# Pairing the sliding-window heads of an even block on both row halves of TensorE

## The chip, the core and the metric

The kernel runs on one core of a Trainium2 chip. A core has TensorE (PE, with its weight loads shown apart as PEld), VectorE (DVE), ScalarE (ACT), GpSimd (POOL) and a queue engine (SP) that only issues DMAs here. The metric is the device time of one execution in microseconds; the numbers given are medians over runs.

## The reference

Four layers run one after another on x of 512 tokens by 1024 channels, in float32: an even attention block, an odd attention block, a convolution block and a gated recurrent block, the last two each followed by an MLP. The change is in the even block alone:

```python
z = h @ w_in          # splits: cq 384, ckv 256, kr 32, sq 512, sk 128, sv 128, gate 1024
o_mla = mla_attention(q_nope, q_rope, k_nope, k_rope, v_mla)      # 8 heads, causal, 512 channels
q_s = apply_rope(z_sq.reshape(b, s, 8, 64)); k_s = apply_rope(z_sk.reshape(b, s, 2, 64))
o_swa = swa_sink_attention(q_s, k_s, v_s, sinks)                  # 8 heads of 64, window 128
o = jnp.concatenate([o_mla, o_swa], axis=-1) * jax.nn.silu(z_gate)
y = o @ w_out
```

In the sliding-window attention (SWA) heads 0 to 3 share the first key and value head and heads 4 to 7 the second. A query block of 128 tokens sees its own and the previous block, and a sink joins the softmax's sum.

## The kernel before

Matrices are multiplied as three products each: both operands are split into a high and a low part, and high*high, high*low and low*high are added up in PSUM (`mm3`, L206). `wgran` (L210) loads a piece of a weight by a DMA on SP's queue into `raw` (4 buffers), ACT copies the high part and DVE or POOL subtracts to get the low part into `hl` (5 buffers).

o lies transposed, eight chunks of 128 channels by 512 tokens: chunks 0 to 3 hold the MLA heads in pairs, 4 to 7 the SWA heads in pairs. `gates` (L703) computes one chunk of silu(z_gate) into o: eight steps of three products of 512 columns, then Tanh on ACT and one DVE operation. When a chunk's attention is done, `pv_out` (L690) multiplies it in.

Attention is a generator that yields after each step: one pair of heads and one query block. A step computes the scores of either head (`scores`, L694, three products into one of two PSUM tiles "sc"), the softmax (`softmax`, L629: a DVE pass with mask and minimum, Exp on ACT, a reciprocal on DVE, the scaling on POOL), the transposes of the probabilities on PE (`p_T`, L662, copied out by ACT), and the products with V (`pv_pair`, L680, two heads side by side on column halves).

`mla()` has 16 steps, with 128 to 512 keys; `swa()` has 16 steps, with 128 or 256 keys. In SWA before the change the pairs are heads (0,1), (4,5), (2,3), (6,7). Queries are stored as tiles that hold head i on partitions 0 to 63 and head i+4 on partitions 64 to 127, keys likewise; a step of before uses two such tiles and one row half of each, and V of one key head for both.

`weave` (L260) mixes a main generator with fill, which is here the gates of chunks 1 to 3, the key and value product (`ev_sk`), and the gates of chunks 4, 6, 5, 7. After step i it lets the fill go on until a cost of `cost*(i+1)/n` units is issued; a gate's step of three products counts 1, a step of the key product 0.5. What it issues for step i may not run before the last PE instruction of step i-FD (`behind`, with `FD = 6`); for i < FD there is no such hold:

```python
marks.append(self.last(self.pe))
with self.behind(marks[-1 - FD] if i >= FD and FD >= 0 else None):
    have = self.advance(fill, have, want(i + 1) - 1e-6)
```

The first weave spends `W_MLA` = 52 units on MLA, the second the rest of 76 on SWA. The order of the instructions on each engine is fixed when the program is built, by a planner that simulates the time line and takes what is ready by priority; on the chip each engine runs its list in that order. Modulation sums for later layers (`ada`, DVE lines L544 and L546, 512 KB loads on SP's queue) are released by `tick` at the ends of gates and heads. After SWA, `out_first` (L734) splits o and multiplies it with w_out (`gemm_tb`, L318), whose rows are in the order of o's channels.

Of the kernel before, what the change touches and what calls it, by code (L numbers as in the profile page):

```python
# [16 lines left out]
P = 128  # L17
# [3 lines left out]
KC = D // P  # L21
EPS = 1e-6
BIG = 1e30
TERMS = ((0, 0), (0, 1), (1, 0))
# [5 lines left out]
C_SM = C_CM + 512  # L30
# [9 lines left out]
STRICT = 0  # L40
FD = 6
ADA_OFF = 0
W_MLA = 52
ONDVE = (0, 1, 2)
W_FOX = 3
MAIN_OFF = 0
# [18 lines left out]
SQF = 0  # L65
G0 = 2
# [41 lines left out]
def cap4(v, o):  # L108

    return bass.AP(tensor=v.tensor, offset=v.offset + o, ap=[[P, 4], [0, 32], [1, P]])  # L110


class K:
# [96 lines left out]
    def wgran(self, w, k0, nk, c0, cw, own=False):  # L210

        n = nk * cw
        raw = self.wp.tile([P, 1024], F32, tag="raw", name=self.nm("raw"), bufs=4)
        self.nc.sync.dma_start(
            out=raw[:, :n].rearrange("p (k c) -> p k c", c=cw),
            in_=w[k0 * P:(k0 + nk) * P, c0:c0 + cw].rearrange("(k p) c -> p k c", p=P))
        if own:
            hl = self.work("hl2", [P, 2, 1024], F32R)
        else:
            hl = self.wp.tile([P, 2, 1024], F32R, tag="hl", name=self.nm("hl"), bufs=5)  # L220
        hi, lo = hl[:, 0, :n], hl[:, 1, :n]
        self.nc.scalar.copy(out=hi, in_=raw[:, :n])  # L222
        self.wn += 1
        eng = self.nc.gpsimd if self.lo_pool and self.wn % self.lo_pool == 0 else self.nc.vector
        eng.tensor_tensor(out=lo, in0=raw[:, :n], in1=hi.bitcast(F32), op=ALU.subtract)  # L225
        return hl[:, :, :n].rearrange("p a (k c) -> p a k c", c=cw)
# [33 lines left out]
            have += c  # L260
        return have

    def weave(self, main, n, fill, cost):


        have, marks = 0, []
        want = cost if callable(cost) else lambda i: cost * i / n
        for i in range(n):
            with self.rank(-MAIN_OFF):
                next(main)  # L270
            marks.append(self.last(self.pe))
            with self.behind(marks[-1 - FD] if i >= FD and FD >= 0 else None):
                have = self.advance(fill, have, want(i + 1) - 1e-6)
        self.run(main)

# [418 lines left out]
    def scores(self, rows, q, k, qb, k0, n, extra=None):  # L694
# [5 lines left out]
            self.nc.tensor.matmul(ps[:, :n], lhsT=A[:, qb * P:(qb + 1) * P], rhs=Bh[:, k0:k0 + n], start=False, stop=True)  # L700
        return ps

    def gates(self, act, w, c0, o, cs):  # L703

        nc = self.nc
        for c in cs:
            def e(m, ps, oc=o[:, c, :]):
                nc.scalar.activation(out=oc, in_=ps, func=AF.Tanh, scale=0.5)
                nc.vector.scalar_tensor_tensor(out=oc, in0=oc, scalar=1.0, in1=ps, op0=ALU.add, op1=ALU.mult)
            yield from self.gemm_ws(act, w, c0 + c * P, P, KC, e)  # L710
# [54 lines left out]
    def even(self, act, gs):  # L765
        nc, h = self.nc, self.h
        w = h["ev_w_in"][0]
# [36 lines left out]
        SV = self.work("SV", [P, NTB, P])  # L804
# [9 lines left out]
        o = self.otile()  # L814
# [7 lines left out]
        for c in range(5):  # L822
            ps = self.psum("tp")
            for tb in range(NTB):
                nc.tensor.transpose(ps[:, tb * P:(tb + 1) * P], lat[tb][:, c * P:(c + 1) * P], self.ident)
            s = self.vcol("ev_q_norm", c) if c < 3 else self.vcol("ev_kv_norm", c - 3)
# [10 lines left out]
        V = [self.work("V", [P, 512]) for _ in range(NTB)]  # L837
# [49 lines left out]
        def swa():  # L887
            self.npool = NPL[1]
            t = self.tmp()[:, :512].rearrange("p (tb d) -> p tb d", d=P)
            nc.scalar.dma_start(out=t, in_=sqd[:, 8:10, :].rearrange("(tb p) n d -> p tb (n d)", p=P))  # L890
            kT = self.heads_T(t, 128, lambda s, tb: s[:, tb])

            def load(i):
                t = self.tmp()[:, :512].rearrange("p (tb r d) -> p tb r d", r=2, d=64)
                for r in range(2):
                    nc.scalar.dma_start(out=t[:, :, r, :], in_=sqd[:, i + 4 * r, :].rearrange("(tb p) d -> p tb d", p=P))
                return self.heads_T(t, 128, lambda s, tb: s[:, tb].rearrange("p r d -> p (r d)"), -0.125)

            qTs = {0: load(0), 1: load(1)}
            for hd in (0, 4, 2, 6):  # L900
                r = hd // 4
                pv = self.psum("pv")
                for qb in range(NTB):
                    k0 = max(0, qb - 1)
                    nb = qb - k0 + 1
                    n = nb * P
                    ps = []
                    for h_ in (hd, hd + 1):
                        sc = self.scores(slice(64 * r, 64 * r + 64), qTs[h_ % 4], kT, qb, k0 * P, n)
                        ps.append(self.softmax(sc, n, self.cst[:, C_SM + 256 - n:C_SM + 256], sink=self.nsink[:, h_:h_ + 1]))  # L910
                    self.pv_pair(pv, [[SV[:, b, r * 64:r * 64 + 64] for b in range(k0, qb + 1)]] * 2, ps, qb)
                    if hd == 4 and qb < 2:
                        qTs[qb + 2] = load(qb + 2)
                    yield
                self.tick(TSW)
                self.pv_out(o[:, 4 + hd // 2, :], pv)

        def fill():
            if SQF:
                yield from self.gates(act, w, 1440, o, (0, 1)[G0:])  # L920
                yield from self.gemm_xs(act, w, 1184, 256, KC, ev_sk)
                yield from self.gates(act, w, 1440, o, (2,))
                yield from self.gemm_xs(act, w, 672, 512, KC, ev_sq)
                yield from self.gates(act, w, 1440, o, (3, 4, 6, 5, 7))
                return
            yield from self.gates(act, w, 1440, o, (1, 2, 3))
            yield from self.gemm_xs(act, w, 1184, 256, KC, ev_sk)
            yield from self.gates(act, w, 1440, o, (4, 6, 5, 7))

        self.lo_pool = LOP[0]  # L930
        if not SQF:
            self.run(self.gates(act, w, 1440, o, (0,)))
        g = fill()
        self.weave(mla(), 16, g, W_MLA + 16 * SQF)
        self.weave(swa(), 16, g, (96 - 8 * G0 if SQF else 76) - W_MLA)
        return o


# [710 lines left out]
def build(tc, h, upto=99):  # L1649
    nc = tc.nc  # L1650
    with ExitStack() as es:
        k = K(tc, h, es)
        k.epsc = k.cp.tile([P, 1], F32, name="epsc")
        nc.vector.memset(k.epsc, EPS)
        x_in = h["x"][0]
        out = h["out"][0]
        x1 = k.dp.tile([T, D], F32, name="x1")
# [4 lines left out]
        with k.scope(t4=5, xn=1, SB=2, wide=8, wsb=2, rep=1, prow=1, col=1):  # L1662
            cc, cc2, act, gs = k.start(x_in, h["c"], h["c_2"], wa[0], ba[0], h["g_pre"][0], h["ev_w_in"][0], 384)
# [30 lines left out]
                        k.mark()  # L1694
                    return o

        act = first(0, lambda a: k.even(a, gs), act, x_in, out if upto == 1 else x1, h["ev_w_out"][0], t4=4, ru=1, s=6, pt=6, b4=6, V=4, SV=1)
        if upto == 1:
            return
        act = first(1, k.odd, act, x1, out if upto == 2 else x2, h["od_w_out"][0], t4=2, ru=1, hn=1, s=6, pt=6, b4=4, Vd=4, V=4, foxA=1, foxB=1, foxBh=2, lp=1)  # L1700
# [63 lines left out]
        with tc.tile_pool(name="xp", bufs=1, reuse_waits="tile") as k.xp:  # L1764
            act, xr = second(0, act, k.conv, x2, t4=4, u=3, dw=1, dwr=1, w4=1, u4=4, dg=3)
# [27 lines left out]
        with tc.tile_pool(name="xp", bufs=1, reuse_waits="tile") as k.xp:  # L1793
            act, xr = second(1, act, k.hgrn, x4, V=8, X=3, F=1, op=2, hn=1, gt=1, AT=1, Ad=2, T0=1, T1=1, T2=1, T3=1, T4=1, T5=1, T6=1)
# [41 lines left out]
```

## Time and profile before

| | |
|---|---|
| median of 3 runs | 2090.42 us (2090.31 to 2091.31) |
| profiled execution | 2096.67 us, of which its span, first to last instruction, is 2094.5 us |
| mean granted TensorE clock | 0.964 of full speed |
| busy: PE, DVE, ACT, POOL | 94%, 65%, 41%, 36% of the span |

The rows of the next section are from that profiled execution. Times there are microseconds from the start of the span. An engine is busy while it executes; matmuls are pipelined, and the ends shown overlap the next one, so that the time of a run of products is best read from its start to the start of what follows.

### The profile page before, as it was taken

What the parts mean: (1) busy time and instruction counts of PE and PEld (TensorE: products, weight loads), DVE (VectorE), ACT (ScalarE), POOL (GpSimd) and SP (SyncE); (2) the same over time, 40 slices, a digit from 0 to 9 for tenths busy, and PEclk for the clock granted to TensorE, in tenths of its full rate; (3) what the DMA queues carried; (4) which work ended last, traced back from release to release, by engine and by line L of the source; (5) the groups of instructions that cost most, each with busy time, mean ns of one, the idle gap of its engine ahead of it and who ended that gap; (6) DMA issues with size and microseconds to landing.
All of it is one profiled execution on the core that took longest, in us unless ns stands there. A gap on an engine that the chain in (4) does not pass through costs nothing. (4 is left out here: it accounts for less than half of the span.)

```text
span 2094.5 us, 33197 instructions
## 1 busy us (share of the span) xinstructions
PE 1958.5 (94%) x13047; PEld 1598.5 (76%) x13047; DVE 1356.8 (65%) x1992; ACT 862.1 (41%) x1465; POOL 745.2 (36%) x671
## 2 busy tenths in 40 slices
PE   7799999689999999889899999999989998999998
PEld 5687767677766787458787989877777678898896
DVE  4356774467553379546987648668777958475673
ACT  4245542235543342143525436244445534353452
POOL 1233334233233333006242322456666443323232
PEclk9899979899999999989999999999999999999999
DMA  8475456377761335832555225353313422242331
GB/s 306 134 211 154 131 175 150 80 173 166 116 149 50 129 123 187 226 82 80 174 166 165 80 91 181 127 150 109 100 58 113 132 81 72 90 131 71 121 100 62
DMA packets 229971, 272.12 MB, mean 130 GB/s; under 512 B 26810, under 2 KB 154009, under 8 KB 229816
## 3 DMA queue, kind: packets, MB, share of 16 engines
q1 hardware_dynamic: 192054, 232.83, 38.5%
q10 hardware_dynamic: 37762, 37.18, 6.0%
q8 instruction: 103, 1.69, 0.3%
q14 instruction: 52, 0.43, 0.1%
HBM read 253.57 MB, written 16.40 MB: 129 GB/s over the span
## 5 line engine op out<-in xcount | busy, mean ns | idle before, releaser
L208 PE MATMUL mm<-hTh,hl 128*128 128x512 f32 (+2 forms) x1200 | 371.8, 384 | 0.1
L222 ACT CAST hl<-raw 128x1024 fp32r<-128x1024 f32 (+3 forms) x219 | 224.2, 1033 | 242.3 <-PE mm L208 121.4
L208 PE MATMUL mm<-hl,hid 128*128 128x512 f32 x1344 | 317.4, 395 | 3.6 <-DVE hid L201 2.0
L208 PEld LDWEIGHTS mm<-hl,hid 128*128 128x128 f32 x1344 | 251.7, 188 | 64.0 <-DVE hid L201 2.8
L225 DVE TENSOR_TENSOR hl<-raw,hl 128x1024 fp32r<-128x1024 f32 (+2 forms) x187 | 246.6, 1328 | 56.2 <-ACT hl L222 55.5
L208 PEld LDWEIGHTS mm<-hTh,hl 128*128 128x128 f32 (+1 forms) x1200 | 217.4, 188 | 49.0 <-issue 6.5
L208 PE MATMUL mm<-hl,hTh 128*128 128x256 f32 (+3 forms) x848 | 220.9, 342 | 31.5 <-DVE t L625 20.6
L208 PE MATMUL mm<-hTl,hl 128*128 128x512 f32 (+2 forms) x600 | 229.3, 382 | 0.1
L208 PEld LDWEIGHTS mm<-hl,hTh 128*128 128x128 f32 x848 | 153.6, 202 | 49.0 <-issue 15.0
L1148 POOL TENSOR_TENSOR xr<-xr,t 128x512 f32<-128x512 f32 x56 | 80.9, 1445 | 307.8 <-DVE t L1145 307.8
L644 POOL TENSOR_TENSOR s<-s,sm 128x256 f32<-128x256 f32 (+3 forms) x112 | 80.6, 720 | 201.0 <-DVE sm L640 192.7
L546 DVE SCALAR_TENSOR_TENSOR acc<-araw,ccol,acc 128x512 f32<-128x512 f32 x154 | 134.8, 875 | 26.6 <-DMA araw<-in_ada_w_dram 20.6
L208 PE MATMUL mm<-hl,hTl 128*128 128x256 f32 (+3 forms) x424 | 143.3, 338 | 0.7 <-DVE hTl L458 0.7
L200 ACT CAST hl<-raw 128x1024 fp32r<-128x1024 f32 x84 | 86.8, 1048 | 138.5 <-PE mm L208 111.9
L201 DVE TENSOR_TENSOR hl<-raw,hl 128x1024 fp32r<-128x1024 f32 x84 | 131.4, 1579 | 13.8 <-ACT hl L200 13.2
L208 PEld LDWEIGHTS mm<-hTl,hl 128*128 128x128 f32 (+1 forms) x600 | 112.9, 188 | 22.0 <-issue 1.7
L1211 POOL TENSOR_TENSOR raw<-raw,raw 128x1024 f32<-128x1024 f32 x28 | 77.1, 2752 | 143.1 <-DVE rows L1211 89.2
L225 POOL TENSOR_TENSOR hl<-raw,hl 128x1024 fp32r<-128x1024 f32 x32 | 80.9, 2529 | 88.6 <-ACT hl L222 88.5
L1145 DVE TENSOR_TENSOR t<-mm,rows 128x512 f32<-128x512 f32 x56 | 38.5, 688 | 108.7 <-PE mm L208 108.3
L639 ACT ACTIVATE s<-s,sm 128x256 f32<-128x256 f32 (+5 forms) x128 | 69.6, 544 | 90.1 <-DVE sm L637 83.5
L1596 POOL TENSOR_TENSOR X<-X,T 128x512 f32<-128x512 f32 x56 | 76.3, 1368 | 58.0 <-ACT op L1556 45.1
L208 PE MATMUL sc<-b,b 64*128 64x256 f32 (+7 forms) x384 | 92.0, 356 | 1.7 <-DVE sm L637 1.3
(366 smaller groups left out, 4060.0 us busy)
## 6 DMA issues: line engine op xcount, KB each, us to landing
raw<-in_mlp_w_dram SPq DMA_DIRECT2D x128, 512.0 KB
araw<-in_ada_w_dram SPq DMA_DIRECT2D x72, 512.0 KB
raw<-in_hgrn_w_in_dram SPq DMA_DIRECT2D x40, 512.0 KB
araw<-in_w_ada_dram SPq DMA_DIRECT2D x32, 512.0 KB
raw<-in_od_w_in_dram SPq DMA_DIRECT2D x32, 512.0 KB
raw<-in_ada_w_dram SPq DMA_DIRECT2D x24, 512.0 KB
rows<-row SPq DMA_DIRECT2D x16, 512.0 KB
raw<-in_conv_w_in_dram SPq DMA_DIRECT2D x16, 512.0 KB
```

Of the source, the lines that this page charges most:

```text
L200: nc.scalar.copy(out=hi, in_=src)
L201: nc.vector.tensor_tensor(out=lo, in0=src, in1=hi.bitcast(F32), op=ALU.subtract)
L208: self.nc.tensor.matmul(out, lhsT=lt[a], rhs=rt[b], start=start and n == 0, stop=stop and n == 2)
L222: self.nc.scalar.copy(out=hi, in_=raw[:, :n])
L225: eng.tensor_tensor(out=lo, in0=raw[:, :n], in1=hi.bitcast(F32), op=ALU.subtract)
L546: eng.scalar_tensor_tensor(out=acc, in0=raw[:, k], scalar=c, in1=acc, op0=ALU.mult, op1=ALU.add)
L639: nc.scalar.activation(out=s[:, :m], in_=s[:, :m], func=AF.Exp, scale=-1.0, bias=mn, accum_out=sm)
L644: nc.gpsimd.tensor_tensor(out=p, in0=p, in1=r.to_broadcast([P, n]), op=ALU.mult)
L1145: nc.vector.tensor_tensor(out=t, in0=ps, in1=G[:, n * 512:(n + 1) * 512], op=ALU.mult)
L1148: eng.tensor_tensor(out=xs, in0=xs, in1=t, op=ALU.add)
L1211: eng.tensor_tensor(out=out, in0=x, in1=y, op=f)
L1596: nc.gpsimd.tensor_tensor(out=xk, in0=xk, in1=cap(Tt, 1, [(row - 1, 2), (2, nb), (0, hh)]), op=ALU.mult)
```

## The change

SWA's pairs become (i, i+4) for i = 0 to 3. Both heads of a pair lie in one query tile, on its two row halves. `scores_pair` issues their six products alternately, one on rows 0 to 63 into one PSUM tile, one on rows 64 to 127 into the other, and only then come the two softmaxes. One query tile is loaded ahead instead of two. V of both key heads is used in a step.

The chunks 4 to 7 of o now hold heads (0,4), (1,5), (2,6), (3,7). So that gate and output weights fit, `Paired` reads the columns of w_in's gate part for chunks 4 to 7 in two pieces of 64 columns, and the rows of w_out from 512 on in two pieces of 64 partitions, with two DMAs for each piece of weight instead of one. The gates of 4 to 7 are issued in order.

`W_MLA` goes from 52 to 44, so that SWA gets 32 units instead of 24, and the second weave holds the fill of step i behind step i-2 instead of i-6. A setting that was not in use (`SQF`) is removed.

```diff
-W_MLA = 52
+W_MLA = 44
...
+class Paired:
+    def __init__(self, w, n0, rows):
+        self.w, self.n0, self.rows = w, n0, rows
+    def pieces(self, k0, nk, c0, cw):
+        w, n0 = self.w, self.n0
+        if self.rows:
+            if k0 * P < n0:
+                return [(slice(0, P), slice(0, cw), w[k0 * P:(k0 + nk) * P, c0:c0 + cw].rearrange("(k p) c -> p k c", p=P))]
+            i = (k0 * P - n0) // P
+            return [(slice(64 * r, 64 * r + 64), slice(0, cw),
+                     w[n0 + 256 * r + 64 * i:n0 + 256 * r + 64 * (i + nk), c0:c0 + cw].rearrange("(k p) c -> p k c", p=64))
+                    for r in range(2)]
+        i = (c0 - n0) // P
+        return [(slice(0, P), slice(64 * r, 64 * r + 64),
+                 w[k0 * P:(k0 + nk) * P, n0 + 256 * r + 64 * i:n0 + 256 * r + 64 * i + 64].rearrange("(k p) c -> p k c", p=P))
+                for r in range(2)]
...
+        rv = raw[:, :n].rearrange("p (k c) -> p k c", c=cw)
+        if isinstance(w, Paired):
+            for ps, cs, src in w.pieces(k0, nk, c0, cw):
+                self.nc.sync.dma_start(out=rv[ps, :, cs], in_=src)
...
-    def weave(self, main, n, fill, cost):
+    def weave(self, main, n, fill, cost, fd=FD):
...
-            with self.behind(marks[-1 - FD] if i >= FD and FD >= 0 else None):
+            with self.behind(marks[-1 - fd] if i >= fd and fd >= 0 else None):
...
+    def scores_pair(self, q, k, qb, n, extra=None, k0=0):
+        pss = [self.psum("sc") for _ in range(2)]
+        for t, (a, b) in enumerate(TERMS):
+            for r, ps in enumerate(pss):
+                rows = slice(64 * r, 64 * r + 64)
+                self.nc.tensor.matmul(ps[:, :n], lhsT=q[rows, a, qb * P:(qb + 1) * P], rhs=k[rows, b, k0:k0 + n],
+                                      start=t == 0, stop=t == 2 and extra is None)
...
-            qTs = {0: load(0), 1: load(1)}
-            for hd in (0, 4, 2, 6):
-                r = hd // 4
+            nxt = load(0)
+            for i in range(4):
+                qT = nxt
...
-                    ps = []
-                    for h_ in (hd, hd + 1):
-                        sc = self.scores(slice(64 * r, 64 * r + 64), qTs[h_ % 4], kT, qb, k0 * P, n)
-                        ps.append(self.softmax(sc, n, self.cst[:, C_SM + 256 - n:C_SM + 256], sink=self.nsink[:, h_:h_ + 1]))
-                    self.pv_pair(pv, [[SV[:, b, r * 64:r * 64 + 64] for b in range(k0, qb + 1)]] * 2, ps, qb)
-                    if hd == 4 and qb < 2:
-                        qTs[qb + 2] = load(qb + 2)
+                    ps = [self.softmax(sc, n, self.cst[:, C_SM + 256 - n:C_SM + 256], sink=self.nsink[:, h_:h_ + 1])
+                          for sc, h_ in zip(self.scores_pair(qT, kT, qb, n, k0=k0 * P), (i, i + 4))]
+                    self.pv_pair(pv, [[SV[:, b, r * 64:r * 64 + 64] for b in range(k0, qb + 1)] for r in range(2)], ps, qb)
+                    if qb == 1 and i < 3:
+                        nxt = load(i + 1)
...
-                self.pv_out(o[:, 4 + hd // 2, :], pv)
+                self.pv_out(o[:, 4 + i, :], pv)
+        wp = Paired(w, 1440 + 512, False)
...
-            yield from self.gates(act, w, 1440, o, (4, 6, 5, 7))
+            yield from self.gates(act, wp, 1440, o, (4, 5, 6, 7))
...
-        self.weave(swa(), 16, g, (96 - 8 * G0 if SQF else 76) - W_MLA)
+        self.weave(swa(), 16, g, 76 - W_MLA, 2)
...
-        act = first(0, lambda a: k.even(a, gs), act, x_in, out if upto == 1 else x1, h["ev_w_out"][0], t4=4, ru=1, s=6, pt=6, b4=6, V=4, SV=1)
+        act = first(0, lambda a: k.even(a, gs), act, x_in, out if upto == 1 else x1, Paired(h["ev_w_out"][0], 512, True), t4=4, ru=1, s=6, pt=6, b4=6, V=4, SV=1)
```

## Rows read from the trace of the kernel before

**Rows 1.** The page's head and its part 1: busy us (share) and instructions.
```profile
span 2094.5 us, 33197 instructions
...
PE 1958.5 (94%) x13047; PEld 1598.5 (76%) x13047; DVE 1356.8 (65%) x1992; ACT 862.1 (41%) x1465; POOL 745.2 (36%) x671
```

**Rows 2.** Stretches of MLA and SWA: length, busy us (instructions) by engine, clock, DMA.
```profile
154.00:163.00 9.00, 5.60 (x29) 4.01 (x27) 7.04 (x15) 2.87 (x8) 0.97 (x2) 0.82 0.61 162
163.00:187.00 24.00, 23.95 (x172) 20.10 (x171) 15.28 (x50) 13.30 (x36) 7.99 (x12) 0.92 0.50 154
251.30:275.80 24.50, 24.35 (x151) 16.10 (x150) 17.38 (x54) 12.48 (x40) 10.55 (x25) 1.00 0.37 112
275.80:282.50 6.70, 5.81 (x37) 3.79 (x36) 6.70 (x20) 4.62 (x13) 3.78 (x8) 1.00 0.80 221
282.50:309.80 27.30, 27.30 (x122) 17.10 (x122) 17.40 (x51) 11.29 (x38) 10.89 (x21) 0.50 0.49 144
```

**Rows 3.** PE by line and shape from 130 to 163 us: busy, mean ns.
```profile
L208 PE MATMUL mm<-hTh,hl 128*128 128x512 f32 x56 | 18.2, 397 | 0.0
```

**Rows 4.** The same view from 163 to 242.5 us.
```profile
L208 PE MATMUL mm<-hTh,hl 128*128 128x512 f32 x50 | 17.1, 407 | 0.0
...
L208 PE MATMUL mm<-hl,hTh 128*128 128x256 f32 x64 | 15.1, 314 | 0.0
```

**Rows 5.** The same view from 242.5 to 310 us.
```profile
L208 PE MATMUL sc<-b,b 64*128 64x256 f32 x72 | 17.0, 357 | 0.4 <-DVE sm L637 0.4
L208 PE MATMUL mm<-hTh,hl 128*128 128x512 f32 x22 | 8.2, 417 | 0.0
...
L208 PE MATMUL sc<-b,b 64*128 64x128 f32 x24 | 5.1, 325 | 0.0
```

**Rows 6.** PE in order of time in SWA: start, us, what.
```profile
253.28 0.61 PE L208 MATMUL sc<-b,b 64*128 64x256 f32 x3
253.83 0.43 PE L686 MATMUL pv<-pt,SV 128*64 128x128 f32 x2
...
255.47 0.55 PE L208 MATMUL sc<-b,b 64*128 64x128 f32 x3
255.95 0.44 PE L686 MATMUL pv<-pt,SV 128*64 128x128 f32 x4
...
263.40 0.62 PE L208 MATMUL mm<-hTh,hl 128*128 128x512 f32 x2
...
264.09 0.64 PE L208 MATMUL mm<-hTh,hl 128*128 128x512 f32 x2
...
284.50 1.01 PE L208 MATMUL sc<-b,b 64*128 64x256 f32 x3
285.43 0.69 PE L667 MATMUL tp<-cst,s 128*128 128x128 f32 x2
```

**Rows 7.** The same view at MLA's start and at the first output product.
```profile
155.77 0.64 PE L654 MATMUL tq<-cst,t 128*96 128x128 f32 x4 [1.43 <-DVE b L201]
...
310.82 0.73 PE L208 MATMUL mm<-hl,oT 128*128 128x512 f32 x2 [0.71 <-ACT oT L200]
```

**Rows 8.** The same view in the odd block's Diff heads.
```profile
468.09 0.96 PE L208 MATMUL sc<-b,b 64*128 64x512 f32 x3
...
500.62 0.97 PE L208 MATMUL sc<-b,b 64*128 64x512 f32 x6
```

**Rows 9.** PE by line and shape from 242.5 to 251.3 us.
```profile
L208 PE MATMUL sc<-b,b 64*128 64x256 f32 x12 | 2.5, 312 | 0.0
L208 PE MATMUL sc<-b,b 64*128 64x128 f32 x6 | 1.1, 290 | 0.0
```

**Rows 10.** DMA queues, 110 to 115.5 and 132.2 to 135.9 us: packets, MB, share.
```profile
q1 hardware_dynamic: 3059, 1.54, 106.7%
...
q10 hardware_dynamic: 2728, 0.75, 113.0%
```

**Rows 11.** Issues of the output weight's loads: ns, first and last start us.
```profile
L214 SPq DMA_DIRECT2D raw<-in_ev_w_out_dram x8: 367/368/478, 147.3 to 261.0; - x8
```

More of the change, by code (lines that the diff above doesn't have):

```diff
@@ L213, in wgran @@
         raw = self.wp.tile([P, 1024], F32, tag="raw", name=self.nm("raw"), bufs=4)
-        self.nc.sync.dma_start(
-            out=raw[:, :n].rearrange("p (k c) -> p k c", c=cw),
-            in_=w[k0 * P:(k0 + nk) * P, c0:c0 + cw].rearrange("(k p) c -> p k c", p=P))
+        rv = raw[:, :n].rearrange("p (k c) -> p k c", c=cw)
+        if isinstance(w, Paired):
+            for ps, cs, src in w.pieces(k0, nk, c0, cw):
+                self.nc.sync.dma_start(out=rv[ps, :, cs], in_=src)
+        else:
+            self.nc.sync.dma_start(out=rv, in_=w[k0 * P:(k0 + nk) * P, c0:c0 + cw].rearrange("(k p) c -> p k c", p=P))
         if own:
@@ L701, in scores @@
         return ps
+    def scores_pair(self, q, k, qb, n, extra=None, k0=0):
[5 more added lines that the diff above has]
+                                      start=t == 0, stop=t == 2 and extra is None)
+        if extra is not None:
+            A, Bhs = extra
+            for ps, Bh in zip(pss, Bhs):
+                self.nc.tensor.matmul(ps[:, :n], lhsT=A[:, qb * P:(qb + 1) * P], rhs=Bh[:, :n], start=False, stop=True)
+        return pss
     def gates(self, act, w, c0, o, cs):
@@ L906, in swa @@
                     n = nb * P
-                    ps = []
-                    for h_ in (hd, hd + 1):
-                        sc = self.scores(slice(64 * r, 64 * r + 64), qTs[h_ % 4], kT, qb, k0 * P, n)
-                        ps.append(self.softmax(sc, n, self.cst[:, C_SM + 256 - n:C_SM + 256], sink=self.nsink[:, h_:h_ + 1]))
-                    self.pv_pair(pv, [[SV[:, b, r * 64:r * 64 + 64] for b in range(k0, qb + 1)]] * 2, ps, qb)
-                    if hd == 4 and qb < 2:
-                        qTs[qb + 2] = load(qb + 2)
+                    ps = [self.softmax(sc, n, self.cst[:, C_SM + 256 - n:C_SM + 256], sink=self.nsink[:, h_:h_ + 1])
[3 more added lines that the diff above has]
+                        nxt = load(i + 1)
                     yield
                 self.tick(TSW)
-                self.pv_out(o[:, 4 + hd // 2, :], pv)
+                self.pv_out(o[:, 4 + i, :], pv)
+        wp = Paired(w, 1440 + 512, False)
         def fill():
[L919 to L925, printed above, removed]
             yield from self.gates(act, w, 1440, o, (1, 2, 3))
             yield from self.gemm_xs(act, w, 1184, 256, KC, ev_sk)
-            yield from self.gates(act, w, 1440, o, (4, 6, 5, 7))
+            yield from self.gates(act, wp, 1440, o, (4, 5, 6, 7))
         self.lo_pool = LOP[0]
-        if not SQF:
-            self.run(self.gates(act, w, 1440, o, (0,)))
+        self.run(self.gates(act, w, 1440, o, (0,)))
         g = fill()
-        self.weave(mla(), 16, g, W_MLA + 16 * SQF)
-        self.weave(swa(), 16, g, (96 - 8 * G0 if SQF else 76) - W_MLA)
+        self.weave(mla(), 16, g, W_MLA)
+        self.weave(swa(), 16, g, 76 - W_MLA, 2)
         return o
```

## The prediction

> **What bounds the kernel now.** I read the page first: TensorE (PE) is busy for 94% of a span of 2094.5 us [rows 1]. The change touches one stage, so I then cut the even block into stretches [rows 2], counted PE's products in each by shape [rows 3 to 5], and read the order of time on PE for what one run of products costs [rows 6]. The reader should see a stage bound by PE in three moods. From 154 to 163 us PE works 5.60 us of 9.00: the MLA attention is starting, the fill (gate and key products, woven in to keep PE busy) has run out, and PE's transposes wait for DVE [rows 7]. From 163 PE is full. At 275.8 the last fill product is done; in the next 6.70 us DVE is busy all the time and PE idles 0.89 us, and from 282.5 to 309.8 PE is full again, but at a granted clock of 0.50, which is the 1.2 GHz level [rows 2]. So the last 27.3 us of the stage run on a half-speed PE, after the fill has dried up.
>
> I count fill in units of three products of 512 columns, as one gate step issues them: 0.69 us each, from 263.40 to 264.09 [rows 6]. Before 163 us there are 28 units (56 products named hTh, two to a unit [rows 3]): 8 of gate 0, 20 of fill. Then 25 units and 32 half-width ones (64 named hl,hTh, the key weights), together 41 [rows 4]. In the SWA stage 11 units are left (22 products) [rows 5]. Together 72: three gates, 16 for the keys, four gates. The code explains the split: fill asked for in step i is held behind step i-6, so the first six steps' fill of each weave is free: 52*6/16 = 19.5, so 20 at the start, and 6*1.5 = 9 of SWA's share already inside MLA, 52+9 = 61 = 20+41.
>
> **The score pairs.** Removed: 32 runs of three products in SWA (24 of 256 columns, 8 of 128 [rows 5]). Added: 16 runs of six, alternating between the two row halves and two PSUM tiles. One run of three, to the start of the next instruction, takes 0.55 us with 256 columns and 0.48 with 128 [rows 6]. What six on both halves cost is shown in the odd block, whose Diff heads have the same form: three products of 512 columns were busy for 0.96 us, six for 0.97 [rows 8]. So a pair costs what one head cost. Saved: 12*0.55 + 4*0.48 = 8.5 us at full clock. The other end: run in turn, six cost 0.55 plus three more streams of 256 columns, (0.96-0.61)/3 = 0.12 us each, so 0.90 for 1.10, and 16*0.20 = 3.2 us. I take 8.5, since the row is of the same shape.
>
> **The held-back gates.** With 44 for 52 and a hold of two steps in SWA, the first six MLA steps free 16.5, so 17 units; MLA as a whole gets 44 plus two SWA steps of 2 units, 48, so 31 after the start; SWA proper gets 24 for 11.
> At the start, three units fewer cover the wait for DVE: PE runs dry 3*0.69 = 2.1 us earlier and nothing else is ready. Cost 2.1 us (0 if the scheduler finds other work).
> In MLA ten units leave (6.9 us). PE was full there and DVE, ACT and POOL were busy 15.28, 13.30 and 7.99 us of 24 [rows 2], so I let the stage shrink by it; the units come back in SWA at the same price. Sum 0.
> In SWA, fill lasts to step 13 of 0 to 15 (44+2*14 = 72) instead of drying up 34 us before the end. The cold 27.3 us would be 27.3/1.69 = 16.1 at full clock (a run of three is 0.93 us cold, from 284.50 to 285.43, and 0.55 warm [rows 6]): 11.2 us saved, and the idle 0.89 too.
>
> **What takes something back.** First, dry steps remain. SWA's own PE work after 251.3 is 58.5 - 11.2 - 0.9 less 11*0.69 = 38.8 us; with 13 pairs cheaper by about 0.53 (six of the 32 runs, 18 products, lie before 251.3 [rows 9]), 31.9 over 13 steps, 2.45 a step. The last fill is released behind step 11, so some 3.5 steps or 8.6 us are dry. Before, the clock fell 6.7 us after the last fill; the 1.9 us beyond that cost 1.9*0.69 = 1.3 us. Second, DVE. It worked 17.38+6.70+17.40 = 41.5 us in these 58.5 [rows 2]; with one to two more gates to split and gate it needs some 44 of about 48. In the stretch where it was full PE lost 13% (0.89 of 6.70); I take that for a third of 48 us: 2 us (0 to 6). ACT worked 12.48+4.62+11.29 = 28.4 us and POOL 25.2 in the same stretches; both still fit under 48 and hide. Third, both score tiles now belong to one pair, so the next pair waits until DVE has read both heads; behind that wait on PE stand transposes, PV products and fill of earlier steps, in an order fixed beforehand. That is inside the 2 us.
>
> **Weights and queues.** Gates 4 to 7 are now loaded as two DMAs each of 64 columns: packets of 256 bytes for 512. A 512-byte packet took 16*5.5*1.067/3059 = 30.7 ns of one engine, one of 256 bytes 16*3.7*1.130/2728 = 24.5 ns (writes, the nearest row) [rows 10]. So 512 KB takes 2048*24.5/16 = 3.1 us for 1024*30.7/16 = 2.0, and four gates 4.7 us more of a DMA system that is full just then, with the reads for MLA's first heads on the other queue. PE has fill to about 152 us (154 less 2.1) and the wait that follows ends on DVE [rows 7], so I take 0.5 us of 0 to 4.7. Four of the eight output weight loads are halved by partition, packets unchanged; they are issued from 147.3 to 261.0 us [rows 11], 50 us before the first output product [rows 7], and their eight parts, with the gates' four extra issues, delay nothing that is due. One query load fewer at the start of SWA is covered by the end of MLA.
> The Trainium skill speaks against this part: "DMA: Bandwidth & Descriptors", section Specifications, asks for at least 512 bytes per transfer for line rate. The rows agree in direction (98 ns per KB of one engine in packets of 256 bytes, 61 in packets of 512). If the smaller packet took as long as the larger one, an estimate from that rule, the four gates would take 7.9 us more for 4.7, and the forecast would move by about 0.3.
>
> **Sum.** -8.5 - 11.2 - 0.9 + 2.1 = -18.5; +1.3 +2.0 +0.5 give -14.7. The profiled execution took 2096.67 us (span 2094.5), 6.25 above the median of 2090.42; the sum is of its span, so 2081.97 for such an execution and 2090.4 - 14.7 = 2075.7 for the median. Behind the stage the output products start when the last PV tile is out, and they run on PE alone, so the shift is kept.
>
> **Rivals.** (1) The clock falls again well before the end, since two units a step are thin: the 11.2 is lost with the 1.3, and -14.7 + 11.2 - 1.3 = -4.8: 2085.6. For it: the clock fell in this very stage. Against: it held from 251.3 to 282.5 with only 11 units of fill [rows 2, 5]. Chance 0.18. (2) The halves run in turn: 5.3 less, 2081.0. Against it [rows 8]. Chance 0.05. (3) Slower: MLA starves. If its steps are held by their own chains, the 6.9 us of fill taken out is not recovered (-7.8 left), and PE's gaps let the clock fall there as they do from 154 to 163 (0.82). MLA's own work from 163 to 242.5 is 79.5 us less 25*0.69 and 32*0.35 (half-width units, taken at half), 51; each warm us costs 0.69 more when cold. From 11 us of it cold the change loses; with half, 25 us, it is +9.5: 2100. For it: the dip at 154 to 163; against: PE was full and no other engine above 64% in the stretch shown [rows 2]. Chance 0.14, of which 0.02 within 0.2%. (4) The gain is given back behind the stage, because modulation sums that filled DVE in the slow stretch come due later: about 2089. Chance 0.04.
>
> **Chances and range.** The forecast has 0.59, its own range 2072 (nothing taken back) to 2084 (DVE and the loads at their upper ends: -18.5+1.3+6+4.7 = -6.5). 0.2% is 4.2 us, about what a measurement of this kernel can tell from no change. Faster: 0.59 + 0.05 + 0.12 of rival 1 = 0.76. Same: 0.06 + 0.02 + 0.04 = 0.12. Slower: 0.12. The range runs from 2069, with the idle at the start better filled than I think, to 2091, which leaves out rival 3's upper part and a little below.
>
> **What would show it.** Six products of 256 columns on the score tiles in about 0.55 us; about 24 units of fill in SWA; a clock of 1.00 to within a few us of the stage's end, and the first output product some 14 us earlier than 310.8 [rows 7]; PE full in MLA. Wrong if the clock column shows 0.50 over many us in SWA or in MLA, or if six products take 0.9.

## The result and the profile after

The change made the kernel slower: 2124.37 us median (2113.43 to 2129.68) for 2090.86, a ratio of 1.0139, 95% interval [1.0113, 1.0165]. The forecast was 2075.7. All ratios with an interval, here and below, are estimated over the fast runs alone (one run of e10, of 6415 us, and one of e15, of 3101 us, were slow), and are not quotients of the medians, which would give 1.0160 here. The profiled execution took 2113.43 us, the quickest of its four, so that it shows little more than half of the loss; two more profiles, of 2121.56 and 2125.10 us, stand further down (e13, e16). The page's head and part 1, to compare with [rows 1]: PE does the same products in the same time, in a span 16.8 us longer.

```profile
span 2111.3 us, 33205 instructions
...
PE 1959.9 (93%) x13047; PEld 1599.2 (76%) x13047; DVE 1357.4 (64%) x1992; ACT 860.6 (41%) x1465; POOL 748.3 (35%) x671
```

Where the 16.8 us are is read from four marks on PE's list: the starts of the first MLA score, of the first output product, of the first product of the odd block, and of the last PV product of that block's Diff heads (its heads that take the difference of two softmaxes):

| | MLA starts | output | odd block | Diff ends | span |
|---|---|---|---|---|---|
| before | 154.12 | 310.82 | 364.2 | 583.0 | 2094.5 |
| after | 155.51 | 316.84 | 375.1 | 599.1 | 2111.3 |
| later by | 1.4 | 6.0 | 10.9 | 16.1 | 16.8 |

So the stage that was to win 14.7 us loses 6.0, the output stage 4.9 more, the odd block 5.2 more. Four profiles of the change, this one, e5, e13 and e16, have the output mark at 315.5 to 319.5 and the odd block at 374.1 to 378.8, so that 2 us between two marks of single profiles say little. Stretches of after, to compare with [rows 2] (length, busy us and instructions by engine, clock, DMA); the last two are MLA and SWA, each from its first score product on:

```profile
154.00:163.00 9.00, 6.34 (x25) 4.60 (x26) 5.95 (x12) 2.42 (x6) 0.83 (x1) 0.57 0.87 250
163.00:187.00 24.00, 24.00 (x152) 19.40 (x150) 12.01 (x40) 13.12 (x35) 6.39 (x10) 0.88 0.38 107
...
220.00:236.00 16.00, 12.12 (x91) 8.48 (x89) 12.00 (x29) 8.48 (x22) 3.39 (x4) 1.00 0.79 221
...
282.50:309.80 27.30, 24.83 (x147) 15.75 (x146) 19.53 (x53) 13.54 (x41) 8.91 (x20) 0.94 0.64 172
...
155.51:241.54 86.03, 80.21 (x536) 62.55 (x536) 59.94 (x162) 43.80 (x117) 29.43 (x34) 0.92 0.58 165
241.54:316.84 75.30, 67.20 (x401) 44.61 (x402) 45.17 (x139) 35.64 (x113) 27.84 (x67) 0.95 0.38 106
```

The same two stretches of before:

```profile
154.12:242.80 88.68, 85.18 (x567) 66.82 (x565) 64.11 (x166) 46.55 (x121) 25.67 (x38) 0.96 0.57 168
242.80:310.82 68.02, 66.13 (x371) 43.17 (x370) 47.46 (x144) 34.67 (x109) 29.71 (x63) 0.80 0.42 121
```

The clock did as forecast there: 0.94 for 0.50 in the stretch from 282.5. But PE, idle for 3.50 and 1.89 us in the two stages of before, is now idle for 5.82 and 8.10: in MLA's last steps (12.12 of 16 us busy from 220), and at SWA's end. PE's order of time (start, duration, engine, line, operands, count, and in brackets the idle time ahead and what ended it), to compare with [rows 6, 7]:

```profile
286.57 0.61 PE L733 MATMUL sc<-b,b 64*128 64x256 f32 x3
287.11 0.44 PE L691 MATMUL tp<-cst,s 128*128 128x128 f32 x2
287.48 0.43 PE L710 MATMUL pv<-pt,SV 128*64 128x128 f32 x2
287.84 0.62 PE L733 MATMUL sc<-b,b 64*128 64x256 f32 x3
...
313.81 0.69 PE L691 MATMUL tp<-cst,s 128*128 128x128 f32 x2 [4.78 <-POOL s L668]
...
316.84 1.22 PE L229 MATMUL sc<-hl,oT 128*128 128x512 f32 x2 [0.71 <-ACT oT L221]
...
349.16 2.07 PE L229 MATMUL mm<-hl,oT 128*128 128x512 f32 x4 [6.46 <-DVE t L794]
...
512.67 0.55 PE L691 MATMUL tp<-cst,s 128*128 128x128 f32 x3 [4.08 <-DVE s L1074]
```

First, the score products still come in runs of three: all 32 runs of the stage do. In the rows shown a pair's two heads start 1.27 us apart, with transposes and PV products between. A pair's products alternate in the program, but the planner takes for each engine what is ready first, and side by side they never are. That the second PSUM tile comes free later than the first is the likely reason: in e6 below, whose products are bound to one order, PE issues one product and the other five come 1.0 to 4.5 us later in 14 of the 16 pairs.

Second, three long waits are new: 4.78 us at the end of SWA, 6.46 us at the output and 4.08 us in the odd block. DVE's list shows what the first two stand on:

```profile
306.35 0.48 DVE L661 CUSTOM_DVE_ANT_0 s<-sc,cst,nsink 128x256 f32<-128x256 f32 x1
...
310.96 1.54 DVE L570 SCALAR_TENSOR_TENSOR acc<-araw,ccol,acc 128x512 f32<-128x512 f32 x2 [4.12 <-DMA araw<-in_ada_w_dram]
312.41 0.15 DVE L664 RECIPROCAL sm<-sm 128x1 f32<-128x1 f32 x1
...
346.90 1.54 DVE L570 SCALAR_TENSOR_TENSOR acc<-araw,ccol,acc 128x512 f32<-128x512 f32 x2 [17.54 <-DMA araw<-in_w_ada_dram]
348.36 1.40 DVE L794 SCALAR_TENSOR_TENSOR t<-mm,sm,rows 128x512 f32<-128x512 f32 x2
```

A modulation sum (`acc`) waits for its weights, and the list is kept in order: the last softmax's reciprocal at 312.41 and the evacuation of the first output tiles at 348.36 stand behind it. SP's queue shows why the second load was late (issue time, duration of the issues), and SP's own waits from 300 to 352 us (total, times, longest) what it stood behind:

```profile
326.63 15.97 SPq L534 DMA_DIRECT2D row<-arow  x4
342.70 0.91 SPq L519 DMA_DIRECT2D araw<-in_w_ada_dram  x2
...
SPq L534 <- DMA raw<-in_od_w_in_dram: 12.2, 1, 12.2
```

Four row stores ahead of it held the queue for 15.97 us, 12.2 of them because one store waited until a weight load of the odd block had landed. Before has such a wait on the queue too (15.3 us), but the sums ahead of the evacuation had ended by then, and the evacuation came without a wait of PE:

```profile
321.02 0.75 DVE L546 SCALAR_TENSOR_TENSOR acc<-araw,ccol,acc 128x512 f32<-128x512 f32 x1
330.64 1.41 DVE L756 SCALAR_TENSOR_TENSOR t<-mm,sm,rows 128x512 f32<-128x512 f32 x2 [8.87 <-POOL sm L389]
```

With the gates held back, the `tick` that releases the sums comes later too: the last six loads of the odd block's sums are issued from 314.5 to 352.7 us, before from 297.2 to 321.8.

The wait is not all of the output stage's loss. Before had a wait of 4.40 us there, on POOL, which is gone. Between the two marks idle time grew by 2.0 us and busy time by 2.9, at a clock of 0.89 for 0.94:

```profile
310.82:364.20 53.38, 48.80 (x208) 39.28 (x209) 24.02 (x31) 17.18 (x32) 19.45 (x23) 0.94 0.65 160
316.84:375.10 58.26, 51.68 (x216) 40.78 (x217) 31.23 (x39) 17.37 (x32) 20.04 (x22) 0.89 0.67 170
```

The third wait, in the odd block, is of another kind:

```profile
507.90 1.40 POOL L1143 TENSOR_TENSOR hn<-hn,o 128x512 f32<-128x512 f32 x1 [2.91 <-ACT hn L1141]
508.08 1.23 DVE L1073 TENSOR_TENSOR sm<-sm,nlam 128x1 f32<-128x1 f32 x1
...
509.86 2.34 POOL L249 TENSOR_TENSOR hl<-raw,hl 128x1024 fp32r<-128x1024 f32 x1 [0.56 <-ACT hl L246]
509.90 2.71 DVE L1074 SCALAR_TENSOR_TENSOR s<-s,sm,s 128x384 f32<-128x384 f32 x1
```

Two DVE operations of the softmax ran beside operations of POOL that had begun before them. The first, a product of one column, took 1.23 us for 0.14 in before. The second, which subtracts one softmax from the other, took 2.71 and ended 0.4 us after the POOL subtraction that had begun 0.04 us ahead of it. Together they are 3.2 us longer than in before, of a wait of 4.08. In before the same two begin in the other order, DVE first, and DVE takes 0.60:

```profile
498.55 0.60 DVE L1043 SCALAR_TENSOR_TENSOR s<-s,sm,s 128x384 f32<-128x384 f32 x1
498.61 2.79 POOL L225 TENSOR_TENSOR hl<-raw,hl 128x1024 fp32r<-128x1024 f32 x1 [1.26 <-ACT hl L222]
```

Here too the clock has a share. From the transposes that start the Diff heads to their last product, idle time grew by 2.2 us and busy time by 3.0:

```profile
448.05:583.00 134.95, 132.18 (x771) 105.01 (x772) 91.89 (x215) 64.98 (x134) 43.81 (x37) 0.99 0.72 138
458.96:599.13 140.17, 135.15 (x771) 107.03 (x772) 91.79 (x215) 65.09 (x134) 43.52 (x37) 0.96 0.70 134
```

### The profile page after: what moved, and what is told of

Its sections match the earlier page's. It is cut to its first block, busy times and chain, and to the rows that moved or that the text cites. A ratio compares the mean times of both kernels' runs of the same rounds, so it can differ in the third digit from the quotient of the medians.

```text
span 2111.3 us, 33205 instructions
## 1 busy us (share of the span) xinstructions
PE 1959.9 (93%) x13047; PEld 1599.2 (76%) x13047; DVE 1357.4 (64%) x1992; ACT 860.6 (41%) x1465; POOL 748.3 (35%) x671
## 5 line engine op out<-in xcount | busy, mean ns | idle before, releaser
L246 ACT CAST hl<-raw 128x1024 fp32r<-128x1024 f32 (+3 forms) x219 | 224.0, 1033 | 243.7 <-PE mm L229 123.1
L668 POOL TENSOR_TENSOR s<-s,sm 128x256 f32<-128x256 f32 (+3 forms) x112 | 83.1, 744 | 203.2 <-DVE sm L664 199.3
L222 DVE TENSOR_TENSOR hl<-raw,hl 128x1024 fp32r<-128x1024 f32 x84 | 127.2, 1527 | 13.8 <-ACT hl L221 13.2
L229 PEld LDWEIGHTS mm<-hl,hTl 128*128 128x128 f32 x424 | 85.4, 201 | 8.6 <-DVE hTl L482 1.6
```

The costliest lines, as they stand in the source:

```text
L222: nc.vector.tensor_tensor(out=lo, in0=src, in1=hi.bitcast(F32), op=ALU.subtract)
L229: self.nc.tensor.matmul(out, lhsT=lt[a], rhs=rt[b], start=start and n == 0, stop=stop and n == 2)
L668: nc.gpsimd.tensor_tensor(out=p, in0=p, in1=r.to_broadcast([P, n]), op=ALU.mult)
```

## The experiments

Ratios are to the kernel before, with 95% intervals; marks are from one profiled execution each, as above. Every edit makes the planner draw new lists, so a ratio holds the price of the new lists beside that of the edit.

| run | ratio | output | odd block | Diff ends | span |
|---|---|---|---|---|---|
| e1 pairs alone | 1.0033 [1.0014, 1.0051] | 317.6 | 368.5 | 585.1 | 2103.5 |
| e2 hold alone | 1.0053 [1.0033, 1.0072] | 311.8 | 371.0 | 589.5 | 2104.9 |
| e3 whole loads | 1.0073 [1.0048, 1.0099] | 318.2 | 377.3 | 595.4 | 2106.2 |
| e4 sums held | 1.0051 [1.0033, 1.0069] | 316.7 | 367.0 | 590.9 | 2101.1 |
| e5 after again | 1.0146 [1.0123, 1.0169] | 319.5 | 378.8 | 600.5 | 2110.3 |
| e6 chained | 1.0093 [1.0073, 1.0113] | 321.6 | 375.1 | 596.8 | 2105.5 |
| e7 hold, sums held | 1.0053 [1.0038, 1.0069] | 313.4 | 363.0 | 581.5 | 2099.6 |
| e8 44 alone | 1.0106 [1.0088, 1.0124] | 332.0 | 382.6 | 604.7 | 2120.3 |
| e9 40 for 44 | 1.0057 [1.0040, 1.0074] | 307.1 | 371.7 | 594.1 | 2106.5 |
| e10 two steps, sums held | 1.0054 [1.0035, 1.0073] | 307.4 | 357.7 | 587.4 | 2097.5 |
| e11 sums held alone | 1.0023 [1.0008, 1.0038] | 310.7 | 361.6 | 582.1 | 2092.4 |
| e12 chained, 52, sums held | 1.0025 [1.0009, 1.0042] | 312.1 | 363.5 | 585.2 | 2103.0 |
| e14 40, sums held | 1.0028 [1.0007, 1.0048] | 309.1 | 364.4 | 587.8 | 2102.2 |
| e15 40, sums held, chained | 1.0059 [1.0037, 1.0080] | 321.3 | 371.5 | 592.3 | 2105.4 |

**The parts by themselves.** e1 is the change with the fill as before, e2 the kernel before with the fill of the change. The edit of e1 against the change (e2 has the other values, in the kernel before):

```diff
-W_MLA = 44
+W_MLA = 52
...
-        self.weave(swa(), 16, g, 76 - W_MLA, 2)
+        self.weave(swa(), 16, g, 76 - W_MLA)
```

> Only the new pairs and their split loads; W_MLA is 52 and the hold six steps as before. Theory A (the loss comes from holding the gates back, which brings the modulation sums later): within 4 us of before, near 2091, since the fixed order on PE keeps the two heads' products apart, as in the profile after, so the pairs save nothing. Theory B (the split loads of 64 columns cost it): about 2105 or more. The forecast's own view (pairs save 8.5 us): near 2082.

> Only W_MLA 44 and the hold of two steps, on the pairs and loads of before. Theory A: slower by most of the loss, 2105 to 2125. Theory B: near 2091 or under, as the gates then keep the clock up.

Either part alone is slower, so theory A, which had e1 within 4 us of before, falls for the pairs; e2's median, 2107.60 us, lies in its range, but 0.53% is not most of the loss. e1's SWA takes 72.2 us for 68.0 with the same clock (0.80) and the same fill. Its waits (total, times, longest) show the pair's price: both score tiles belong to it, and PE waits 2.1 us for DVE to read them, where before waited 0.4. At the end of the Diff heads 2.1 us of e1's loss are left; the rest of it in this profile, 6.9 us, lies behind them.

```profile
PE sc L733 <- DVE sm L661: 2.1, 4, 0.7
```

e2 reaches the output products at 311.8 with the clock up, and then has the wait on DVE behind late sums:

```profile
PE mm L208 <- DVE t L756: 5.0, 1, 5.0
```

**The split loads.** e3 loads gate and output weights whole, so heads meet other heads' gate columns and output rows. The gates' part of its edit:

```diff
-            yield from self.gates(act, wp, 1440, o, (4, 5, 6, 7))
+            yield from self.gates(act, w, 1440, o, (4, 5, 6, 7))
```

> The changed kernel with the gate weights of chunks 4 to 7 and the output weights loaded whole as before, so that the paired heads meet columns and rows of other heads; everything else is kept. Theory A: as the changed kernel, 2112 to 2130. Theory B: back to 2091 or under.

The stage and the output wait are those of the change (7.4 us at 351), so the split loads cost nothing up to the odd block, and theory B falls. In total e3 is still 0.66% quicker than the change, clear of both intervals. In its profile the gain is in the Diff heads. The planner ordered them otherwise, and there POOL's subtraction meets a sum; PE waits 2.49 us for the operation behind it, for 4.08 in the change:

```profile
507.21 2.48 POOL L249 TENSOR_TENSOR hl<-raw,hl 128x1024 fp32r<-128x1024 f32 x1 [0.30 <-ACT hl L246]
507.49 2.74 DVE L570 SCALAR_TENSOR_TENSOR acc<-araw,ccol,acc 128x512 f32<-128x512 f32 x1
...
511.04 1.52 PE L701 MATMUL pv<-pt,Vd 128*128 128x128 f32 x6 [2.49 <-DVE o L1144]
```

So an edit that costs nothing in its own stage moved the total by more than half a per cent.

**The sums held behind the output stage** (`-MK = 3`, `+MK = 11`): in the change (e4), with the hold alone (e7), in the kernel before as a control (e11). The setting also holds the sums of the layers behind in the same way, behind the odd block's output stage.

> The changed kernel, with the odd block's modulation sums held on DVE behind the even block's output stage. Theory A: the wait of PE of 6.5 us in the output stage (DVE waits there 17.5 us for a load of such a sum) goes, and the time falls by 5 to 10 us, to 2105 to 2118, if the sums are not missed later. Theory B: no change.

> The kernel before with the gates held back (44 for 52, two steps for six in SWA) and with the odd block's modulation sums kept behind the output stage on DVE. Held back alone, the run before this one gave 1.0053 with a wait of 4.95 us at the output products at 344 us. Theory A (what the hold-back loses is lost to those sums): the wait is gone and the ratio falls by 5 us to 1.002 to 1.004. Theory B (it is lost because MLA has too little fill): the ratio stays at 1.004 to 1.007.

> The kernel before with nothing but the odd block's sums kept behind the output stage. It is the control of the runs that hold them there. No wait of PE on the output evacuation stands in the profile of before, so both theories expect no gain from it: 0.998 to 1.004, more if the sums are then late in the odd block.

In e4 and e7 the output wait is gone and the odd block starts 8 us earlier. In the change that is worth its price: 1.0051 for 1.0139. In e4 the wait at the end of SWA stays, at 3.65 us: the sum that it stands behind is not one of those held. In e7 the ratio is that of e2, against theory A: 8 us gained at the odd block's start, 5.3 kept in the span. And e11 starts the odd block 2.6 us sooner than before and is 0.23% slower. Some of that is seen to be paid in the odd block, where the held sums stand on DVE among the rotations of queries and keys: the wait of PE for these grows from 11.9 us (before) to 13.9 (e11), from 12.2 (after) to 14.0 (e4) and from 12.2 (e2) to 13.8 (e7). The rest is not located. e7 has its 8 us still at the end of the Diff heads, and behind them the lists of e2 and e7 on PE and DVE are the same, so that what its span loses there is not the order of the lists.

**Products side by side.** e6 chains a pair's six products, so that PE issues one alone and then five; e5 is the change again, beside it.

```diff
+        before = None
...
-                self.nc.tensor.matmul(ps[:, :n], lhsT=q[rows, a, qb * P:(qb + 1) * P], rhs=k[rows, b, k0:k0 + n],
-                                      start=t == 0, stop=t == 2 and extra is None)
+                with self.behind(before):
+                    self.nc.tensor.matmul(ps[:, :n], lhsT=q[rows, a, qb * P:(qb + 1) * P], rhs=k[rows, b, k0:k0 + n],
+                                          start=t == 0, stop=t == 2 and extra is None)
+                before = self.last(self.pe)
```

> The changed kernel itself again, so that the next runs can be set against it under the same conditions. Both theories expect a ratio to the kernel before of 1.007 to 1.014, a wait of 4 to 7 us on DVE before the output products at about 349 us, and a wait of 4 to 5 us on POOL at the last transposes of the SWA stage at about 313 us.

> The change with the six score products of a pair chained in program order, so that PE issues one product of the first head alone and then the other five, alternating between the row halves. Theory A (the pairs would pay if their products stood side by side, as six row-half products of the odd block do): the five take about 0.55 us, a pair about 0.85 for 1.08, so 16 pairs save 3 to 4 us and the SWA stage, from its first score product to the first output product, takes 71 to 72 us for the 75.3 of the changed kernel. Theory B (the stage is set by DVE, which reads both score tiles, and by the fill): the stage stays within 1 us of 75. Theory C (row halves of 256 columns run in turn): the five take about 0.8 us.

PE's order of time and its waits in e6:

```profile
280.49 0.62 PE L735 MATMUL sc<-b,b 64*128 64x256 f32 x6
283.91 0.38 PE L735 MATMUL sc<-b,b 64*128 64x256 f32 x1
...
287.56 0.61 PE L735 MATMUL sc<-b,b 64*128 64x256 f32 x5
288.11 0.66 PE L691 MATMUL tp<-cst,s 128*128 128x128 f32 x4
```

```profile
PE sc L735 <- DVE sm L661: 4.6, 6, 2.2
PE tp L691 <- POOL s L668: 3.9, 4, 2.2
```

Where six do stand together they take 0.62 us, and five 0.55 to the next start: two heads for the price of one, as [rows 8] said. But the chain makes the second head's products wait until its tile is read, 4.6 us in the stage, which takes 80.35 us for 75.3. Idle time is only 3.2 us of these 5; busy time grew by 1.9, at a clock of 0.85 in the stage for 0.95. Theory A is right on the products, wrong on the stage. e6 is quicker than e5 only behind it: its output stage takes 53.5 us for 59.3, without the wait behind a late sum. e15 (below) shows the chain once more.

**How much fill to hold back.** e8 is the kernel before with 44 alone, e9 the change with 40, e10 the kernel before with the hold of two steps and the sums held.

> The kernel before with 44 for 52 alone: the hold of six steps stays, so 17 units of fill start MLA, 39 in all its later part and 16 are left for SWA, for 20, 41 and 11. No modulation sum of the odd block then stands on DVE ahead of the first output evacuation. Theory A (the loss is in the sums that come due late): no wait there, five units more in SWA keep the clock up some 8 to 10 us longer, and the ratio is 0.996 to 1.000. Theory B (three units less at MLA's start are what costs): the wait on DVE at 155 us grows from 1.43 to about 3 us and the ratio is 1.001 to 1.004.

> The changed kernel with 40 for 44: four units of fill less in MLA, four more in SWA. Theory A (MLA starves at its end, and in most executions the clock falls there: the changed kernel was profiled in its fast executions, 2112 and 2113 us at a mean clock of 0.962 and 0.965, while most take 2124 to 2130 at 0.955 to 0.957): the dip after 220 us grows, the profile shows 0.50 for 15 us or more between 225 and 260 us, and the ratio is 1.015 to 1.025. Theory B (only the late modulation sums cost): the clock stays up in MLA, and the ratio is that of the changed kernel, 1.013 to 1.016, or less by the clock kept up in SWA.

> The kernel before with the hold of SWA's fill at two steps for six (52 stays) and the odd block's sums behind the output stage: MLA keeps its start of 20 units, gets 35 later and SWA 17 for 11. Theory A: PE's dip at MLA's end is smaller than with 31 units (PE busy 6.5 of 8 us from 220 to 228 there), the cold stretch at the end of SWA shrinks from 27 to some 15 us, and the ratio is 0.997 to 1.001. Theory B (any unit taken out of MLA costs more than it gives in SWA): 1.002 to 1.006.

Both theories miss e8: no wait behind a sum at the output, yet 1.0106. MLA runs dry at its end (first row, 5.51 of 8 us busy), and from there the clock is at 0.50; over SWA, from 248.90 to 331.95, it is 0.74 for 0.80 in before:

```profile
236.00:244.00 8.00, 5.51 (x41) 3.94 (x39) 6.51 (x15) 4.11 (x12) 1.28 (x3) 1.00 0.66 185
244.00:252.00 8.00, 7.83 (x28) 5.58 (x29) 3.73 (x16) 5.09 (x15) 4.65 (x10) 0.50 0.24 66
```

This is rival 3's mechanism, a dry MLA and then a clock that falls, but most of its price lies in SWA (83.1 us for 68.0; MLA 94.9 for 88.7), where rival 3 put it in MLA. e9 then goes against theory A, and further down than theory B allowed for: with still less fill in MLA the stage ends at 307.1, 3.7 us ahead of before, and loses that at the output, where PE waits 9.9 us behind sums:

```profile
341.74 3.12 DVE L570 SCALAR_TENSOR_TENSOR acc<-araw,ccol,acc 128x512 f32<-128x512 f32 x4 [10.01 <-DMA araw<-in_w_ada_dram]
344.77 1.40 DVE L794 SCALAR_TENSOR_TENSOR t<-mm,sm,rows 128x512 f32<-128x512 f32 x2
```

So the amount of fill taken out of MLA does not by itself set the loss. That the order which the planner makes around it does is an inference: no run changes the order alone. e10 starts the odd block 6.5 us before the kernel before and is 0.54% slower: its Diff heads end at 587.4, 229.7 us after that start, where before takes 218.8.

**What helped, together.** e12 is e6 with 52 for 44 and the sums held; e14 is e9 with the sums held; e15 is e14 with the chain.

> The change with its score products chained (one product, then five on both halves), 52 for 44 with the hold of two steps, and the odd block's sums behind the output stage: everything that the runs so far found to help. Theory A (the loss is MLA's dip and the late sums): no output wait, a smaller dip, 0.997 to 1.003. Theory B (the pair's two score tiles, read by DVE one after the other before the next pair may start, hold PE up by themselves: 4.6 us of waits in the chained run, 1.0 in the changed kernel): 1.003 to 1.008.

> The changed kernel with 40 for 44 and the odd block's modulation sums behind the output stage. With 40 alone the first output product came at 307 us for the 310.8 of before, and PE then waited 9.9 us on the output evacuation that stood on DVE behind late sums. Theory A (that wait is the whole remaining loss): no such wait, the odd block's first product at 357 to 362 us, and 0.996 to 1.001. Theory B (holding the sums back costs as much behind the stage as it saves): 1.002 to 1.005.

> The same with the score products chained (one product, then five on both row halves). Theory A (side by side they save about 0.2 us a pair): 2 to 4 us less than without the chain, 0.995 to 1.000. Theory B (the chain binds a pair's first product to the reading of both score tiles, so PE waits for DVE): 1 to 5 us more than without it.

None beats the kernel before. e12 lies 0.25% above it, at the upper edge of its theory A. e14 has its 9.9 us wait cut to 2.4 in two pieces and starts the odd block at 364.4, where before does; it is 0.28% slower, as theory B has it. In e15 the chain brings the first output product 12 us later (321.3 for 309.1) and makes SWA 9.2 us longer, with 13.0 us of idle time for 3.4; in total it costs 5.0 us by the medians and 6.5 by the ratios, where its theory B gave 1 to 5. Yet e12, which has the pairs, their loads and the chain where e10 has none of them, is 0.29% quicker than e10 in total, though its SWA takes 72.0 us for 68.2; the intervals of the two overlap.

**The spread of the change.**

> One more profile of the changed kernel itself. Both of its profiles so far came from its quickest executions (2113 and 2112 us; the others took 2119 to 2130). Theory A (after MLA's dip from 222 to 236 us the clock may stay or fall, and it falls in most executions): in an execution of over 2120 us the profile shows 0.50 for some 25 us between 228 and 265 us, and the SWA stage starts and ends later. Theory B (the spread is from elsewhere): the clock there is as in the two profiles, 1.00 or a fall of 8 us at most, and the extra time lies behind the even block.

> A second profile of the changed kernel, with the same two expectations as the first: 0.50 for some 25 us between 228 and 265 us in an execution of over 2120 us, or the extra time behind the even block.

Theory A falls. Up to the odd block both look like the first profile (375.1; 374.07 and 376.25), and all four profiles of the change have the same lists. The first difference is behind the wait at 512 us. The clock fell behind it in all four, for a time that differs: by the clock column of the two stretches from 500 to 540 some 3.6 us at 0.50 in the first, 6.8 in e5, 10.4 in e13 and in e16. In e13 and e16 it fell once more near 620. Stretches of after, then of e16:

```profile
500.00:520.00 20.00, 15.50 (x94) 12.60 (x93) 13.39 (x24) 12.14 (x24) 5.44 (x4) 0.91 1.00 218
520.00:540.00 20.00, 20.00 (x102) 15.29 (x102) 13.92 (x32) 8.42 (x19) 3.59 (x4) 1.00 0.50 84
620.00:640.00 20.00, 20.00 (x119) 14.11 (x118) 11.85 (x29) 8.45 (x21) 8.84 (x10) 1.00 0.45 137
```

```profile
500.00:520.00 20.00, 15.85 (x94) 12.71 (x93) 13.08 (x22) 11.59 (x22) 4.58 (x3) 0.86 0.95 207
520.00:540.00 20.00, 20.00 (x98) 15.97 (x97) 10.62 (x27) 6.39 (x16) 3.85 (x3) 0.88 0.35 86
620.00:640.00 20.00, 20.00 (x91) 13.28 (x92) 8.76 (x25) 7.99 (x18) 9.89 (x9) 0.74 0.39 80
```

Before has 20.00 at 1.00 in all three. e16's Diff heads take 227.1 us from the odd block's start, after's 224.0, before's 218.8. So in these four the gap of 4.1 us costs its length, and with it go 3 to 10 us at half the clock; what decides how long from one execution to the next stays open. Behind the Diff heads the four profiles take 1509.8 to 1519.9 us, on the same lists (before: 1511.5), so that a difference of some us in one profile's span alone shows nothing.

## Why the prediction was wrong

**The pairs, -8.5: zero.** This step of the prediction failed first: that a pair's six products would run together, a pair at the cost of one head. The price of six products was right (0.62 us in e6), but on PE's list there are 32 runs of three at 0.61 to 0.62 us, as before, and nothing is saved. That they would be issued together was taken from the source, and no rival said that the planner might part them. What the pairs did bring is the wait for two score tiles, put "inside the 2 us": e1 shows 3 us more idle time in SWA (4.9 for 1.9), and 0.33% in all.

**The clock, -11.2 and -0.9, with +1.3: right in the way, a fifth short in size.** SWA's busy time rose from 66.13 to 67.20 us though it now holds 39 more fill products (72 for 33), at 0.23 each 9.0 us; the rest fell by 7.9 for the 9.9 forecast. The fill was as counted: 24 units in SWA, 15 and 32 half-width ones in MLA. It ended at 298.4, some 15 us ahead of the last transposes. The clock fell again at the stage's end, and the output stage has 0.89 for 0.94.

**MLA, 0: wrong.** 31 fewer fill products at 0.23 are 7.1 us, and busy time fell by 5.0. The 2.1 between fit the clock at the start: by the clock column of the rows from 154 to 187 some 14 us at 0.50, for 7 before. Idle time grew by 2.3. The stage shrank by 2.65 us for the 6.9 that I let it.

**DVE near full, +2.0: the resource was right, the mechanism not.** SWA's idle time rose by 6.2 us, of which 4.78 is one wait: a late load in front of a reciprocal in DVE's list. No run takes this wait away by itself, so it is read from the list alone. DVE was not full (45.17 of 75.30 us). The prediction asked what stands behind a stall for the score tiles and not for the sums, whose release hangs on the fill.

**Split loads, +0.5: nothing seen in the stage.** With whole loads, e3, the first output product comes no sooner (318.2 for 316.8). The rule of the Trainium skill, "DMA: Bandwidth & Descriptors", section Specifications, at least 512 bytes a transfer for line rate, shows no price there. The 0.66% that e3 is quicker lie behind the stage in its profile; how much of it is the packets and how much the new lists, no run parts.

**"The shift is kept" behind the stage: wrong, and worth most.** The sum of the stage, -3.9 busy + 8.5 idle + 1.4 start, is the 6.0 of the mark. Behind it come 4.9 at the output, 5.2 in the odd block and 0.7 behind the Diff heads; in e16, nearer to the median, the odd block has 8.3 and the part behind the Diff heads 8.4. The output products do not run on PE alone: their evacuation stood on DVE behind a late sum. Rival 4 had the mechanism, sums that come due later, at 0.04 and only as a gain given back; rival 3 had the sign, at 0.14, with a clock that in the change fell elsewhere. Holding the sums is the largest part that a run took away, 0.9% of 1.4 (e4, measured in another set of runs); in its profile it is 8.2 of the 16.1 us at the end of the Diff heads. The 0.5% that is left is of the size of what the pairs alone (0.33%) or the hold alone (0.53%) cost, and no run divides it further.

## What to carry to other kernels

Where lists are ordered by a planner, look at the list that it makes before pricing products as neighbours: two PSUM tiles that come free apart may part them. When fill is moved, list everything that its steps release, loads and sums of later stages too, and ask which instruction stands behind each in an engine's list. A stage that ends earlier is not a gain until the next stage's list, loads and clock are seen to keep it: e9, e10 and e11 all reached the output products or the odd block sooner than the kernel before, in their profiles, and are slower in total.

## What the runs showed of the hardware

POOL held DVE up: a DVE pass over two SBUF operands that began 0.04 us after a POOL subtraction took 2.71 us for 0.60, a sum in e3 2.74 for 0.75. In before, where DVE began 0.06 us ahead of POOL, DVE took 0.60 and POOL 2.79, for 2.34 in the change. The Trainium skill has this rule in "SBUF — State Buffer", section Who interferes with whom: a DVE instruction with two SBUF inputs and a GpSimd one that reads SBUF contend, and who issues first has the shared port for the whole instruction. The rows agree.

Six products of 256 columns on two row halves took 0.62 us where three on one half took 0.61 to 0.62.
